# Gates and merge of a hybrid decoder trunk by seven half-size products instead of eight

## The chip, the cores and the metric

The kernel runs on one core of a Trainium2 chip. The metric is the device time of one execution in microseconds, the median of three runs. The core has a matrix engine (PE), a vector engine (DVE), a scalar engine (ACT), a general one (Pool), and a queue engine (SP) that issues the transfers between memory and the on-chip buffers.

## What is computed

Two decoder layers on x of 1024 tokens by 1024 channels, all in float32. Four mixers (stick-breaking attention, S5, retention, RG-LRU) work on slices of one input projection; this change concerns the gates, the merge weights and what surrounds them:

```python
h = _rms_norm(x, pre_g)
proj = jnp.einsum('bsd,dc->bsc', h, w_in)
sb_qkv, ssm_u, ret_qkv, lru_u, gates, merge = jnp.split(proj, SPLITS, axis=-1)
# y_sb, y_ssm, y_ret, y_lru from the first four parts
mix = jnp.stack([y_sb, y_ssm, y_ret, y_lru], axis=2).astype(dtype)
mix = mix * jax.nn.silu(gates.reshape(bsz, s, N_BRANCH, BRANCH_WIDTH))
y = jnp.einsum('bsnw,nwd->bsnd', mix, w_branch)
gate = jax.nn.sigmoid(merge.reshape(bsz, s, N_BRANCH, D_MODEL))
merged = jnp.sum(gate * y, axis=2)
out = jnp.einsum('bsd,de->bse', merged, w_out)
return x + _rms_norm(out, post_g)
```

The gates have 4 x 256 columns and the merge weights 4 x 1024, so together 40 tiles of 128 columns out of 1024 channels.

## The kernel before

The work is cut into four units: two layers times two chunks of 512 tokens. A unit streams 64 weight tiles, called fillers: 16 projections (`i < 16`), then for each of the four mixers a group of ten (two gate tiles, eight merge tiles that carry the branch projection of the same columns), then eight tiles of the output projection. A gate or merge tile is 1024 channels by 128 columns; its product with the normalised chunk is 8 k-slices of 128 channels, and each slice takes three passes, since float32 is made of a high and a low float32r part on both sides: high x high, low x high, high x low (`mm3`). Each pass is one matmul of 128 rows by 512 columns, and a tile fills one PSUM bank with 24 of them (`coltile`, and `filler` for the merge).

Weight tiles come through `load_to` (L178), three tiles ahead, into four raw buffers; `split_to` makes the high part on ACT (L86) and the low part on DVE (L89), three half tiles ahead. Every engine works through its queue in the order in which the program was written: the scheduling is manual, and SP issues all transfers in one queue. Position in a unit is counted in halves of fillers, 128 per unit. The mixers and other side tasks are generators that take their steps at the halves listed in the table `PLAN`:

- `prep` builds the S5 tables of a layer, mostly on Pool (L432, L436). Its longest part doubles the rotation tables `tcos` and `tsin` up to 128 columns, with a scratch buffer. In unit 0 it runs from half 2, in unit 1 for the next layer from half 66.
- `prologue_t` (unit 0) and `prologue` (other units) normalise the next unit's chunk; they square the elements, sum, take 1/sqrt, scale, and split into `hh` and `hl`. In unit 0 this starts at half 96.
- `lru`, `s5`, `ret` and `sba` are the mixers; `post` adds the residual.

General buffers come from a ring of 36 (`genp`, shown as g), accumulators from 3 PSUM banks (pa) and 5 (pb). A buffer's new user waits until the last reader of its old content is done, whichever engine that is on. After the two q tiles of a unit, ACT makes 16 copies from PSUM and 8 more within the buffers, in one piece, ahead of the next weight split in its queue.

## Time and profile before

| | us |
|---|---|
| median of three runs | 1898.11 |
| lowest and highest run | 1894.95, 1898.5 |
| span of the profiled execution | 1895.3 |
| PE busy | 1838.7 (97%) |
| DVE busy | 1180.3 (62%) |
| ACT busy | 903.4 (48%) |
| Pool busy | 252.1 (13%) |
| memory traffic of SP's queue | 192.38 MB, 29.6% of 16 engines |

A busy time counts the recorded length of instructions. Matmuls overlap, so their price is read from the distance of their starts. A time for one engine means little until one knows who waits for it: idle time of an engine that nobody waits for costs nothing.

### The profile page before, as it was taken

Reading aid. Unit: us, or ns where it says so; the run is one execution under the profiler, and the core shown is the slowest. Engines: PE = TensorE matmul, PEld = TensorE weight load, DVE = VectorE, ACT = ScalarE, POOL = GpSimd, SP = SyncE. Lnnn points to the kernel's source line nnn. Section 1 sums busy time; section 2 is a strip of 40 time slices with the busy share of each in tenths; the row PEclk is TensorE's granted clock in tenths of the full one; section 3 lists DMA queues with packets and bytes.
Section 4 is the critical chain, followed back from the end, with each engine's and each line's share of the span. In section 5 each row is a group of like instructions: output and inputs, shape, how many; then the busy total and the mean of one; then the engine's idle time right before and its main releaser. Section 6 shows DMA issues by size and latency. Waiting matters only on the chain.

```text
span 1895.3 us, 24847 instructions
## 1 busy us (share of the span) xinstructions
PE 1838.7 (97%) x9210; PEld 1506.0 (79%) x9210; DVE 1180.3 (62%) x2101; ACT 903.4 (48%) x1733; POOL 252.1 (13%) x579
## 2 busy tenths in 40 slices
PE   8979999999989999979999999999999899999997
PEld 6768888888878878858888788888888788888886
DVE  7667755454669676735547956655537694776454
ACT  5862443344476443524446744344353855344333
POOL 7872000020000002880300000000000000000001
PEclk9989999999999999989999999999999999999999
DMA  5231232324332221314234313232243322212222
GB/s 181 90 104 56 68 117 98 122 93 152 106 117 95 100 72 58 108 47 150 96 127 156 115 69 109 78 137 99 90 136 131 103 98 87 81 68 78 97 98 105
DMA packets 68857, 193.96 MB, mean 102 GB/s; under 512 B 9600, under 2 KB 18176, under 8 KB 68736
## 3 DMA queue, kind: packets, MB, share of 16 engines
q1 hardware_dynamic: 68736, 192.38, 29.6%
q8 instruction: 72, 1.18, 0.2%
q14 instruction: 49, 0.40, 0.1%
HBM read 179.11 MB, written 12.58 MB: 101 GB/s over the span
## 4 chain that ended last, share of the span: by engine, by line
PE 83%; POOL 8%; ACT 4%; DVE 3%; issue 2%; DMA 0%; SPq 0%; DVEq 0%; POOLq 0%; ACTq 0%
PE pa L101 66%; PE pb L101 15%; POOL g L432 4%; ACT g L86 2%; PE pb L1020 2%; POOL psc L436 1%; DVE g L89 1%; POOL tcos L432 1%; POOL tsin L432 1%; POOL g L436 1%; ACT g L83 1%; DVE wl L89 1%; ACT wh L86 0%; DVE g L98 0%; PE pb L253 0%
## 5 line engine op out<-in xcount | busy, mean ns | idle before, releaser
L101 PE MATMUL pa<-hh,wh 128*128 128x512 f32 x1576 | 629.5, 399 | 27.4 <-ACT wh L86 27.4
L101 PE MATMUL pa<-hh,wl 128*128 128x512 f32 x1576 | 617.6, 392 | 8.0 <-DVE wl L89 8.0
L101 PE MATMUL pa<-hl,wh 128*128 128x512 f32 x1576 | 617.5, 392 | 0.0
L89 DVE TENSOR_TENSOR wl<-raw,wh 128x512 fp32r<-128x512 f32 (+1 forms) x512 | 373.8, 768 | 225.7 <-ACT wh L86 225.2
L89 DVE TENSOR_TENSOR g<-g,g 128x512 f32<-128x512 f32 (+7 forms) x432 | 296.0, 685 | 124.5 <-ACT g L86 104.6
L101 PEld LDWEIGHTS pa<-hh,wh 128*128 128x128 f32 x1576 | 298.9, 190 | 90.9 <-ACT wh L86 29.7
L86 ACT ACTIVATE wh<-raw 128x512 fp32r<-128x512 f32 (+1 forms) x512 | 328.2, 685 | 86.6 <-PE pb L101 41.0
L101 PEld LDWEIGHTS pa<-hh,wl 128*128 128x128 f32 x1576 | 298.0, 189 | 74.2 <-DVE wl L89 10.6
L101 PEld LDWEIGHTS pa<-hl,wh 128*128 128x128 f32 x1576 | 298.6, 189 | 58.4 <-DVE hl L89 0.2
L83 ACT ACTIVATE g<-pa 128x512 f32<-128x512 f32 x161 | 96.2, 597 | 501.0 <-PE pa L101 464.6
L89 DVE TENSOR_TENSOR g<-g,pa 128x512 f32<-128x512 f32 x128 | 87.6, 684 | 185.1 <-PE pa L101 165.8
L101 PE MATMUL pa<-g,wh 128*128 128x512 f32 x544 | 169.2, 391 | 3.6 <-DVE g L98 3.4
L86 ACT ACTIVATE g<-pb 128x512 f32<-128x512 f32 (+4 forms) x163 | 72.6, 472 | 145.8 <-PE pb L101 87.8
L906 POOL MEMSET g<- 128x512 f32 x8 | 4.0, 526 | 949.0 <-PE pb L101 947.8
L101 PEld LDWEIGHTS pa<-g,wh 128*128 128x128 f32 x544 | 102.1, 188 | 28.0 <-DVE g L98 5.0
L86 ACT ACTIVATE g<-g 128x512 fp32r<-128x512 f32 (+2 forms) x152 | 79.1, 521 | 61.7 <-DVE g L89 31.8
L86 ACT ACTIVATE g<-pa 64x128 fp32r<-64x128 f32 (+3 forms) x214 | 86.4, 404 | 45.2 <-PE pa L101 42.8
L101 PE MATMUL pa<-g,wl 128*128 128x512 f32 x272 | 106.1, 390 | 0.0
L83 ACT ACTIVATE g<-pb 128x512 f32<-128x512 f32 (+4 forms) x203 | 87.8, 513 | 22.8 <-PE pb L101 20.1
L101 PE MATMUL pa<-wh,g 128*128 128x512 f32 x256 | 79.6, 392 | 0.0
L101 PE MATMUL pb<-wh,g 128*128 128x512 f32 x256 | 79.2, 391 | 0.0
L89 DVE TENSOR_TENSOR g<-pa,g 128x512 f32<-128x512 f32 x51 | 35.7, 703 | 54.6 <-ACT g L83 34.8
(207 smaller groups left out, 2086.4 us busy)
## 6 DMA issues: line engine op xcount, KB each, us to landing
raw<-in_ws_dram SPq DMA_DIRECT2D x128, 640.0 KB, 3.8
raw<-in_ws_dram SPq DMA_DIRECT2D x127, 512.0 KB, 3.6
g<-x SPq DMA_DIRECT2D x32, 256.0 KB, 6.1
g<-in_xt_dram SPq DMA_DIRECT2D x16, 256.0 KB, 6.0
g<-in_x_dram SPq DMA_DIRECT2D x16, 256.0 KB, 3.1
x<-g SPq DMA_DIRECT2D x16, 256.0 KB, 2.1
out_dram<-g SPq DMA_DIRECT2D x16, 256.0 KB, 2.0
g<-in_rot_dram SPq DMA_DIRECT2D x8, 256.0 KB, 4.4
```

What stands on the lines that cost most here:

```text
L83: act.activation(out, in_, func, **kw)
L86: act.activation(out, in_, AF.Copy, **kw)
L89: dve.tensor_tensor(out, a, b, op=op)
L101: pe.matmul(out, lhsT=lhsT, rhs=rhs, start=start, stop=stop)
L432: pool.tensor_tensor(out, a, b, op=op)
L436: pool.tensor_scalar(out, a, s1, None, op0=op0)
L906: pool.memset(t, 0.0)
L1020: pe.transpose(ps[:, q * P:(q + 1) * P], r[:, q * P:(q + 1) * P], ident)
```

## The change

The 40 gate and merge tiles of a layer are taken as 20 pairs, and each pair is computed for both chunks of the layer at once, as a product of two-by-two blocks: two column tiles, two halves of the channels, two chunks of tokens. In place of eight block products there are seven, in the form that uses four sums of weights (s1 to s4) and four sums of tokens (t1 to t4). Each product is 4 k-slices of three passes, 12 matmuls.

- A layer's first unit now runs 12 projections, five `x` stages, four projections, five more `x` stages, twenty `y` stages, and the output projection. `x` makes two products each for two pairs; `y` makes three products for one pair, adds the earlier ones on DVE and does the branch projection. The second unit runs `z` stages (two products each for two pairs), `g` and `m` stages (gating and branch projection) and the output projection. Products and gates that are needed later are written to memory (`late`, `put_late`) and read back (`fetch`).
- `build` makes the sums of tokens on DVE and splits all of them; it follows the normalisation of the second chunk, which thereby moves from half 96 to half 24 in unit 0 (task `tb`). The splits are written to memory and read back (`load_set`).
- `wsums` makes the sums of weights in memory: SP copies a block of weights (1.31 MB) and Pool issues transfers that add another block to it, 32 in all, each behind the landing of the one it depends on.
- The `hp` buffers go; the ring of general buffers has 56, and 8 raw buffers hold tiles of 512 columns, loaded ten ahead. The pass of `mm3` is unchanged.
- Half of the q copies go to DVE, and the eight copies within buffers are put off by one half (`hooks`). The first unit's squares move from Pool to ACT and DVE. The transposed copies of `prologue` are made in pieces of 128 columns. The LRU's low weights are padded to all 128 rows.
- `PLAN` is rewritten for the new positions.

```diff
...
-    hp = ctx.enter_context(tc.tile_pool(name="hp", bufs=1))
-    rawp = ctx.enter_context(tc.tile_pool(name="rawp", bufs=4))
+    rawp = ctx.enter_context(tc.tile_pool(name="rawp", bufs=NRAW))
...
+        if u % 2 == 0:
+            x = [("x", *q) for q in ps]
+            f = p[:12] + x[:XA] + p[12:] + x[XA:] + [("y", q) for q in qs]
+        else:
+            z = [("z", *q) for q in ps]
+            m = [[("m", n, i) for i in range(4)] for n in range(4)]
+            f = p[:12] + z[:ZA] + p[12:] + z[ZA:8] + [("g", 0), z[8]] + m[0][:2] + [z[9], ("g", 1)] + m[0][2:] + m[1][:3]
+            f += [("g", 2), m[1][3]] + m[2][:3] + [("g", 3), m[2][3]] + m[3]
...
+    def ahead(s):
+        load_to(s + NRAW + 2)
+        split_to(s + 3)
...
+            b12, b22 = hc[k], hc[4 + k]
+            t1, t2 = G(), G()
+            tt(t1, b1[k].bitcast(F32), b1[4 + k].bitcast(F32), ALU.add)
+            tt(t1, t1, b12, ALU.subtract)
+            stt(t2, t1, -1.0, b22, ALU.mult, ALU.subtract)
+            yield 0
+            put("t1", t1, True)
...
             if k < 4:
                 sqs.append(G())
-                pool.tensor_tensor(sqs[k], xk[k], xk[k], op=ALU.mult)
-                if k:
-                    pool.tensor_tensor(sqs[0], sqs[0], sqs[k], op=ALU.add)
+                actv(sqs[k], xk[k], AF.Square)
...
+    def prod(ps, s, t, more=False):
+
+        for k in range(4):
+            mm3(ps, s, k * P, P, False, (t[k], t[4 + k]), not more and k == 0, k == 3, more)
...
+    def fetch_y(u, n):
+        drain(("lru", "s5", "ret", "sb")[n])
+        put_late()
+        for j in range(2):
+            S["yf", n, j] = fetch(yd[n][j], u)
...
+            for k in range(3):
+                half(s + k)
+                ps = A()
+                prod(ps, s + k, S[("t2", "t3", "t4")[k]])
+                t = G()
+                tt(t, ps, v, ALU.add)
+                v = t
+                if k < 2:
+                    late.append(((u2d, u3d)[k][j], t))
...
-            for q_, qd, _, _, z in todo:
+            for q_, _, _, _, z in todo:
                 copy(q_, z, scale=0.125)
-                copy(qd, z, scale=0.125)
+            for _, qd, _, _, z in todo:
+                ts(qd, z, 0.125)
...
+        def add(a, b):
+            pool.dma_start(a, b, accum_op=ALU.add, max_dma_last_dim=5120)
+
+        for n in order(2 * l):
+            s1, s2, s3, s4 = (wsum[l][j][n] for j in range(4))
+            sp.dma_start(s3, wq[l, n, 2])
+            sp.dma_start(s2, wq[l, n, 3])
+            yield 0
+            add(s3, wq[l, n, 0])
+            yield 0
+            add(s2, s3)
...
-NGEN = 36
+NRAW = 8
+XA = 5
+ZA = 3
+NGEN = 56
...
```

Three places of the new order matter below. The first is ACT's queue in unit 0, at the tile after the twelfth projection. Before, splits and the rotary copies stood there (wh is a weight's high part, pa a PSUM bank):

```order
L86 ACTIVATE wh_1135<-raw_998 128x512
L86 ACTIVATE wh_1151<-raw_1052 128x512 [waits DMAHW6_49]
L86 ACTIVATE g_1169<-pa_1132 32x512 [waits PE_49]
L86 ACTIVATE g_1169<-pa_1132 32x512 x3
L86 ACTIVATE wh_1181<-raw_1052 128x512
L86 ACTIVATE wh_1197<-raw_1133 128x512 [waits DMAHW1_49,Activation_49]
```

Now the four squares of the second chunk stand there (L83, g_1419 to g_1427), and the first of them waits for Pool, whose doubling used that buffer as scratch:

```order
L86 ACTIVATE g_1408<-pa_1358 128x512 [waits PE_49]
L86 ACTIVATE wh_1412<-raw_1065 128x512 [waits DMAHW3_49,Activation_49]
L83 ACTIVATE g_1419<-g_1378 128x512 [waits DMAHW2_49,Pool_49]
L83 ACTIVATE g_1421<-g_1379 128x512 [waits DMAHW3_49]
L83 ACTIVATE g_1424<-g_1380 128x512 [waits DMAHW4_49]
L83 ACTIVATE g_1427<-g_1381 128x512 [waits DMAHW5_49]
L86 ACTIVATE g_1442<-pa_1359 128x512 [waits PE_49]
```

The copy of pa_1359, which frees that bank for PE, now stands behind the squares.

The second is SP's queue in unit 1, the second half of the groups. Before, it held loads of the next chunk and weight tiles, freed by DVE:

```order
L229 DMA g_7835<-x_113 128x512 [waits DMAHW3_49]
L229 DMA g_7836<-x_113 128x512 [waits DMAHW4_49]
L264 DMA g_7820<-in_preg_dram 128x512 [waits DMAHW5_49,PE_49]
L264 DMA g_7821<-in_preg_dram 128x512 [waits DMAHW6_49,PE_49]
L178 DMA raw_7858<-in_ws_dram 128x1280 [waits DMAHW7_49,DVE_49]
L178 DMA raw_7914<-in_ws_dram 128x1280 [waits DMAHW0_49,DVE_49]
```

Now it holds spilled products (u, ge, go), mixer results (y) and small weight tiles; g_8668 takes the scratch of the next layer's doubling:

```order
L1211 DMA g_8662<-ge_212 128x512 [waits DMAHW5_49,DMAHW3_49]
L1211 DMA g_8664<-go_232 128x512 [waits DMAHW4_49,PE_49]
L363 DMA y_0_251<-g_8625 128x512 [waits DVE_49]
L363 DMA y_1_252<-g_8626 128x512 [waits DMAHW6_49,Activation_49]
L1211 DMA g_8668<-y_0_249 128x512 [waits DMAHW7_49,Pool_49]
L1211 DMA g_8670<-y_1_250 128x512 [waits DMAHW0_49]
L217 DMA raw_8674<-in_wb_dram 128x512 [waits DMAHW1_49]
L1211 DMA g_8686<-u_8_175 128x512 [waits DMAHW2_49]
L1211 DMA g_8688<-u_9_176 128x512 [waits DMAHW3_49,PE_49]
L217 DMA raw_8705<-in_wb_dram 128x512 [waits DMAHW4_49,DVE_49]
```

The wait for Pool stands ahead of the loads of u_8, u_9 and of all weight tiles that follow.

The third is Pool's queue in unit 0, after the doubling, in the steps that make the chunk inputs' tables. Before:

```order
L432 TENSOR_TENSOR g_1386<-g_446,g_272 128x8x16
L432 TENSOR_TENSOR g_640<-g_640,g_272 128x128 [waits Pool_49]
L432 TENSOR_TENSOR g_1386<-g_1386,g_640 128x8x16 [waits Pool_49]
L432 TENSOR_TENSOR g_1387<-g_640,g_272 128x8x16 [waits DMAHW6_49]
L432 TENSOR_TENSOR g_640<-g_446,g_272 128x128 [waits Pool_49]
L432 TENSOR_TENSOR g_1387<-g_1387,g_640 128x8x16 [waits Pool_49]
L432 TENSOR_TENSOR g_1386<-g_446,g_272 128x8x16
L432 TENSOR_TENSOR g_640<-g_640,g_272 128x128 [waits Pool_49]
```

Now two transfers that add in memory stand among these steps, the second behind the landing of the first; these rows are the end of that stretch:

```order
L503 TENSOR_TENSOR g_1960<-g_672,g_479 128x8x16
L503 TENSOR_TENSOR g_865<-g_865,g_479 128x128 [waits Pool_49]
L503 TENSOR_TENSOR g_1960<-g_1960,g_865 128x8x16 [waits Pool_49]
L503 TENSOR_TENSOR g_1961<-g_865,g_479 128x8x16
L503 TENSOR_TENSOR g_865<-g_672,g_479 128x128 [waits Pool_49]
L503 TENSOR_TENSOR g_1961<-g_1961,g_865 128x8x16 [waits Pool_49]
L1610 DMA ws_1_0_119<-ws_2_0_123 256x1280 [waits DMASW0_49]
L503 TENSOR_TENSOR g_1960<-g_672,g_479 128x8x16
L503 TENSOR_TENSOR g_865<-g_865,g_479 128x128 [waits Pool_49]
L503 TENSOR_TENSOR g_1960<-g_1960,g_865 128x8x16 [waits Pool_49]
```

The steps below the transfer, and those of ACT and DVE that read their results, stand behind that landing.

## Rows read from the trace of the kernel before

**Rows 1.** The page: span, and busy time of each engine.

```profile
span 1895.3 us, 24847 instructions
...
PE 1838.7 (97%) x9210; PEld 1506.0 (79%) x9210; DVE 1180.3 (62%) x2101; ACT 903.4 (48%) x1733; POOL 252.1 (13%) x579
```

**Rows 2.** Timeline of PE at 500 us: start, us, engine, line, operation.

```profile
499.67 0.39 PE L101 MATMUL pa<-hh,wl 128*128 128x512 f32 x1
499.90 0.39 PE L101 MATMUL pa<-hh,wh 128*128 128x512 f32 x1
500.13 0.39 PE L101 MATMUL pa<-hl,wh 128*128 128x512 f32 x1
```

**Rows 3.** Chain of waits, one piece at 892 us: start, us, what.

```profile
892.48 27.22 PE pa L101 x120
```

**Rows 4.** Waits of PE, whole span: us in total, times, longest.

```profile
PE pa L101 <- ACT wh L86: 27.4, 5, 13.4
```

**Rows 5.** The page, costliest groups: one of three passes; count, busy us, mean ns.

```profile
L101 PE MATMUL pa<-hh,wh 128*128 128x512 f32 x1576 | 629.5, 399 | 27.4 <-ACT wh L86 27.4
```

**Rows 6.** Timeline of PE after its longest stops; idle time and releaser in brackets.

```profile
95.02 0.50 PE L101 MATMUL pa<-hh,wh 128*128 128x512 f32 x1 [2.30 <-ACT wh L86]
...
119.12 0.79 PE L101 MATMUL pa<-hh,wl 128*128 128x512 f32 x1 [7.82 <-DVE wl L89]
...
568.92 0.80 PE L101 MATMUL pa<-hh,wh 128*128 128x512 f32 x1 [5.14 <-ACT wh L86]
...
848.38 0.80 PE L101 MATMUL pa<-hh,wh 128*128 128x512 f32 x1 [13.41 <-ACT wh L86]
```

**Rows 7.** Timelines of ACT, Pool and DVE around the S5 tables of both layers.

```profile
95.52 2.40 ACT L86 ACTIVATE g<-pa 32x512 f32<-32x512 f32 x4
...
115.11 1.26 POOL L432 TENSOR_TENSOR tsin<-tsin,g 128x512 f32<-128x512 f32 x1
...
116.41 0.69 DVE L89 TENSOR_TENSOR g<-pa,g 128x512 f32<-128x512 f32 x1 [14.70 <-POOL tsin L432]
...
118.39 1.28 DVE L89 TENSOR_TENSOR wl<-raw,wh 128x512 fp32r<-128x512 f32 x2
...
846.62 1.08 ACT L86 ACTIVATE g<-pb 128x512 f32<-128x512 f32 x2 [23.47 <-POOL tsin L432]
```

**Rows 8.** Stretches: us, busy us of each engine (instructions), PEclk, DMA share, GB/s.

```profile
20.00:118.00 98.00, 86.86 (x382) 68.19 (x380) 60.52 (x120) 71.05 (x149) 85.72 (x235) 0.98 0.24 83
758.30:847.90 89.60, 76.67 (x406) 62.78 (x405) 45.54 (x68) 33.68 (x62) 79.22 (x206) 0.95 0.21 74
10.00:15.00 5.00, 2.03 (x9) 1.37 (x9) 5.00 (x4) 4.42 (x8) 4.84 (x4) 1.00 1.05 397
10.00:20.00 10.00, 6.97 (x29) 5.16 (x29) 10.00 (x10) 8.61 (x15) 9.84 (x8) 1.00 0.96 361
```

**Rows 9.** Rows by shape of DVE and ACT: count, busy us, mean ns.

```profile
L89 DVE TENSOR_TENSOR wl<-raw,wh 128x512 fp32r<-128x512 f32 x256 | 171.4, 700 | 113.0 <-ACT wh L86 112.5
L89 DVE TENSOR_TENSOR g<-g,g 128x512 f32<-128x512 f32 x232 | 166.5, 718 | 14.7 <-ACT g L83 7.2
L89 DVE TENSOR_TENSOR g<-g,pa 128x512 f32<-128x512 f32 x128 | 87.6, 684 | 185.1 <-PE pa L101 165.8 <-ACT g L83 18.5 <-PE pb L1020 0.7
...
L1058 DVE TENSOR_TENSOR_SCAN g<-g,ec,ones 128x511 f32<-128x511 f32 x32 | 41.1, 1283 | 0.0
...
L98 DVE SCALAR_TENSOR_TENSOR g<-g,ss,g 128x512 f32<-128x512 f32 x26 | 19.3, 745 | 0.0
L98 DVE SCALAR_TENSOR_TENSOR g<-pa,g 64x128 fp32r<-64x128 f32 x64 | 18.5, 289 | 25.6 <-ACT g L86 23.8
...
L83 ACT ACTIVATE g<-g 128x512 f32<-128x512 f32 x44 | 25.8, 625 | 22.8 <-DVE g L89 18.0 <-POOL g L432 4.6
```

**Rows 10.** Page: SP queue (packets, MB, share); a weight load (us to landing).

```profile
q1 hardware_dynamic: 68736, 192.38, 29.6%
...
raw<-in_ws_dram SPq DMA_DIRECT2D x127, 512.0 KB, 3.6
```

## What I expect of the change

> **What bounds the kernel now.** I read the page first, then the waits of PE, the timeline of PE, the rows by shape, and last the waits and rows of the other engines at the places that the change touches. The page shows one engine nearly full: PE is busy for 97% of the span [rows 1]. A busy share says little about matmuls that overlap, so the reader should look at their starts: 512-column matmuls start every 0.226 to 0.23 us (499.67, 499.90, 500.13), though each is shown as 0.39 long [rows 2]. The pitch is their price; over a run of 120 that follow each other in the chain of waits it is 27.22 / 120 = 0.2268 us [rows 3]. PE waits for others for some 45 us in all, of which 27.4 us for ACT's splits, in five waits [rows 4]. DVE is busy for 62% [rows 1]. So PE work that goes is time that goes, unless something now hidden comes out.
>
> **The matmuls that go.** Two 128-column tiles of gate or merge weights over two chunks of tokens cost 2 x 2 x 24 matmuls (8 k-slices, three passes). The seven products cost 7 x 12 (4 k-slices, three passes). That is 96 against 84 for each of 20 pairs in two layers, so 480 matmuls fewer: 480 x 0.2268 = **-108.9 us**, all of it from the group in [rows 5] and the two like it for the other passes. The row padding of the LRU's weights and the wider mask matmul differ by a few us of either sign; I take +2. PE: **-107**.
>
> **Waits that go.** In unit 1, 13.41 us of PE's idle time end with ACT [rows 6], and ACT had waited 23.47 us for Pool's tsin [rows 7]. The part of the S5 tables that caused it is now given other places: -13. After the q tiles of each second chunk PE stands for 5.14 us, at 568.92 [rows 6] and again at 1503.78, while ACT makes sixteen copies and more; half of them are moved to DVE and the rest are put behind the next weight split: 2 x 5.1 = -10. Together **-23**.
>
> **New wait in unit 0.** The normalisation of the second chunk (prologue_t) starts at half 24, where it stood at half 96. Its first square on ACT takes over the scratch buffer of Pool's table doubling, so ACT's queue stands until the doubling is done. In the trace Pool works on these tables almost without a gap, 85.7 of 98 us [rows 8], and its last tsin ends at 115.1 + 1.3 = 116.4 us [rows 7]. The tile of halves 24 and 25 had its first copies on ACT at 95.52 [rows 7]; less its 24 matmuls and the wait of 2.30 us at 95.02 [rows 6], half 24 began at about 87 us. Three products of 12 matmuls bring PE to about 95, where it needs a bank that ACT has not read; ACT's queue opens at 116.4 and takes four squares of 0.63 us before that read [rows 9], so PE goes on at about 119: a stall of 24 us. The kernel before lost 7.8 us there, seen at 119.12 [rows 6]. The seven squares and adds that `first` takes from Pool may bring Pool's end forward by up to 7 us; Pool's seven sums of squares then delay the statistics that PE reads by a few us. Bounds +8 and +20; I take **+13**.
>
> **New wait in unit 1.** SP's queue now holds a load of the S5 result whose buffer is the same scratch, in the middle of the merge stage: SP cannot issue it before the doubling is over, and behind it stand the loads of two spilled products and all weight tiles. Pool needs from 758.3 to 847.9 us, 89.6 us, after the exponent's tail [rows 8]; that tail stands at half 59 now, and PE runs out of loaded operands at about half 73, 14 halves later. By the counts of the part on DVE below, 24 halves of this stage take 80 us on PE and 101 on DVE, so 14 take 47 to 59 us, and the stall is 31 to 43 us. Pool's stretch has 79.2 us of work in it; if its waits go, the lower end is 20. I take **+28**, bounds 20 and 43.
>
> **Pool's queue.** The weight sums are DMAs that add in memory, issued by Pool and each waiting for a landing. Two of them stand among the table steps of unit 0, and ACT and DVE wait for steps behind them at halves 45 and 46. Nothing of the kind is in the trace. The nearest row from below is a 512 KB load that lands in 3.6 us [rows 10]; the sums are 1.31 MB, 2.5 times as much, so 9 us for each if nothing overlaps. Bounds 0 and 18; I take **+7**.
>
> **DVE.** Counted from the new instruction order by the durations of [rows 9], DVE gets about 176 more additions that read PSUM (0.684 us), 35 of SBUF tiles (0.718), 40 scaled ones (0.745) and 96 copies of 64 or 128 columns (0.289): 120 + 25 + 30 + 28 = some 200 us on 1180. That is under 1840 in total, so by the mean it is hidden. By stages it is not: in halves 64 to 87 of units 1 and 3 there are 40 PSUM additions, 36 SBUF ones, 35 splits and the scans, 27 + 26 + 25 + 23 = 101 us, against 300 matmuls and 89 small ones, 80 us. Two splits of 0.70 take 1.28 together [rows 7], 0.91 of their sum, so 101 is some 93. In the q tiles' stage it is 33 against 24. So DVE exceeds PE by 13 + 9 = 22 us in each of two units, 44 in all. In unit 1 the 13 lie under SP's stall, and three halves that are split ahead, some 9 us, are used up first in each unit: 44 - 13 - 18 = 13. Bounds 0 and 44; I take **+15**.
>
> **DMA.** The products, the sums of tokens and the sums of weights are put into memory and read back. Payload grows from 192 MB [rows 10] to some 440 MB. At most the queue moved 397 GB/s over 5 us and 361 over 10 us [rows 8]. In unit 0, halves 40 to 71 hold 127 transfers of 0.262 MB, 4 copies and 4 sums of 1.31 MB: 43.8 MB, or 49 if a sum counts twice. That is 110 to 136 us, against 384 matmuls and 140 small ones, some 103 us. By the same count the last 32 halves of the y stage need 93 to 131 us against 88, unit 2's halves 40 to 71 need 104 to 126 against 99, and its y end 86 to 117 against 88; other stages fit. The sum of what does not fit is 17 to 130 us. Two of four sums are not read before the next unit, and weights are loaded ten tiles ahead; a stall elsewhere also gives the queue time. Bounds 0 and 130; I take **+25**, close to the lower end, because the rate at which a sum reads its target appears in no row.
>
> On this the Trainium skill speaks against the change. "DMA: Bandwidth & Descriptors", section Issuing engines are not separate DMA queues, says that transfers from SP and Pool run on the same 16 engines and interleave; here all but a sliver of packets came from one queue, so no run shows it. "Collectives: The Full Stack", section The bandwidth ceiling: the fold count and why AG ≠ RS ≠ AR, says that a reduction is slow because an addition needs two source reads; by that rule the upper ends above would apply, and the time would be the second rival's. No run here shows it.
>
> **The sum.** 1895.3 - 107 - 23 + 13 + 28 + 7 + 15 + 25 = 1853. The median lies 2.8 us above the profiled span, so **1856 us**.
>
> **Rivals.** (1) *The stalls are hidden and the whole saving comes through.* Pool ends its tables earlier than before (it has lost the squares), SP's blocked load finds operands already loaded, and the memory traffic fits: 1895.3 - 107 - 23 + 8 + 20 + 0 + 0 + 0 = 1793, with the median's 2.8 us 1796; with up to 30 us of the other terms left, 1796 to 1826. For it speaks that PE waited only 45 us in all before and that most buffers are more numerous (56 for 36, 8 raw for 4). Against it speaks Pool's continuous stretch [rows 8]. (2) *The DMA engines become the bound.* If a sum occupies the engines twice and copies from memory to memory run no faster than 361 GB/s, the stages above wait 130 us instead of 25: 1856 + 105 = 1961. It makes the kernel slower as soon as the stages wait more than 25 + (1902 - 1856) = 71 us. For it speaks that the queue's demand exceeds the best rate seen in four stages; against it, that PE's longest waits in the trace end with ACT and DVE, not with a transfer [rows 6]. (3) *The saved matmuls do not shorten PE's time*, because the seven products run in half-length groups of 12 with a new bank each: against it, the 120 matmuls of [rows 3] run over several banks at the same pitch. I give it little; 0.2 us lost at each of 280 products would be 56 us, 1912.
>
> **How the numbers follow.** Forecast (1826 to 1886) 0.47; rival 1 0.24; rival 2 0.18; rival 3 and other mixtures above 1886 0.11, of which 0.03 are still faster, 0.05 within 0.2% and 0.03 slower. Of the time outside the range, about 0.05 lies below and 0.13 above, which gives 1795 to 1945. About 0.2% of the time, 4 us, is what a measurement can tell from no change. Faster: 0.24 + 0.47 + 0.03 = 0.74; same 0.05; slower 0.21.
>
> **What would show it.** Right: PE's 512-column matmuls are 480 fewer at an unchanged pitch; a PE gap of 15 to 25 us around 95 to 120 us that ends with ACT, whose wait names Pool; an SP wait for Pool of some tens of us in unit 1's merge stage, with PE idle behind it; DVE over 90% busy in that stage. Wrong: the pitch rises; PE's waits end with DMAs in units 0 and 2, or ACT's splits wait for raw tiles there (rival 2); no gap over 10 us (rival 1).

## The result, and the profile after

The changed kernel takes 2160.78 us in the median of four runs (2154.18 to 2166.76) against 1897.23 us in four runs of the kernel before (1894.95 to 1898.5): 1.139 times as long, 95% interval 1.1362 to 1.1419. The forecast was 1856 us (1826 to 1886), and the time lies above the range and on the other side of the time before.

First the page of the changed kernel: span, busy times, the two DMA queues (packets, MB, share of 16 engines; q1 is SP's, q0 is Pool's), and of its issues those of the weight sums (count, KB each, us to landing).

```profile
span 2156.5 us, 27173 instructions
...
PE 1828.5 (85%) x8730; PEld 1480.7 (69%) x8730; DVE 1361.6 (63%) x2496; ACT 924.7 (43%) x1825; POOL 275.2 (13%) x605
...
q1 hardware_dynamic: 216432, 416.84, 56.3%
q0 software_dynamic: 8704, 41.95, 9.9%
...
ws<-in_wq_dram POOLq DMA_DIRECT2D x16, 1280.0 KB, 13.4
ws<-ws POOLq DMA_DIRECT2D x16, 1280.0 KB, 12.6
```

The matmuls are 480 fewer than in [rows 1], 8730 for 9210, as the arithmetic says; PE is busy for 85% where it was for 97%. So the matmuls are saved, and PE stands still for much more than they took. Who it waits for, over the whole span (us in total, times, longest):

```profile
PE pb L1091 <- DVE g L89: 105.8, 28, 12.2
PE pa L1189 <- DVE g L89: 101.1, 37, 11.3
PE pa L1189 <- ACT g L86: 42.3, 8, 14.2
PE pa L1189 <- DMA g<-xs_t: 25.0, 9, 5.8
```

Before, the one large row was 27.4 us [rows 4]. The matmuls of L1189 are the seven products and all other passes of `mm3`, those of L1091 the small ones of the attention. The first two rows name DVE, which is busy for only 63%; the reader should not stop at them but ask what DVE had waited for. Part of the answer is a transfer (waits of DVE):

```profile
DVE g L89 <- DMA g<-ge: 56.0, 13, 10.4
DVE g L89 <- DMA g<-y: 32.1, 7, 12.4
DVE g L89 <- DMA g<-u: 16.3, 2, 14.0
```

ge, y and u are values that are read back from memory. Nearly all of the waits for ge and y fall in units 0 and 2, whose `y` stages fetch them; u is fetched by the `z` stages, and 14.0 of its 16.3 us are one wait in unit 1 (see the scratch buffer below). Stretches of 50 us in the `y` stages of units 0 and 2 show what holds them up (columns as in [rows 8]: us, busy us of PE, PEld, DVE, ACT, Pool, clock, DMA share, GB/s; the share adds up the times of packets, so it can pass 1):

```profile
450.00:500.00 50.00, 39.01 (x175) 31.17 (x173) 26.64 (x42) 10.72 (x19) 2.14 (x3) 0.90 1.05 317
...
1500.00:1550.00 50.00, 34.89 (x158) 27.70 (x156) 20.54 (x33) 10.62 (x19) 2.68 (x3) 0.89 1.04 315
1550.00:1600.00 50.00, 41.65 (x164) 33.76 (x165) 26.49 (x42) 8.81 (x15) 2.68 (x3) 0.87 1.04 291
```

The DMA engines are full (1.04 and 1.05), at 291 to 317 GB/s where 361 to 397 were seen before [rows 8]; PE is busy for 35 to 42 of 50 us. That is the second rival's picture. It is not the whole of it: in units 1 and 3 no weight sums are made, yet more than half of the lost time lies there.

To place the loss I laid the starts of PE's instructions against the program's order and took, for every eight halves, the time beyond pitch times count. The kernel before has some 56 us of such time in all. After:

| unit | 0 | 1 | 2 | 3 | sum |
|---|---|---|---|---|---|
| us beyond PE's pitch | 129 | 124 | 60 | 107 | 420 |

420 - 56 = 364 more lost time, less 107 for the matmuls: 257 of the 261 us by which the span is longer. The pitch of the small matmuls is uncertain: other choices of it move both sums by some tens of us, single units by up to 20, and the difference by under 10. In the new order units 0 and 2 have 164 halves (the `y` stages are 72 to 147), units 1 and 3 have 104 (`z` stages from 24, the output projection from 88).

### The profile page after: what moved, and what is told of

Read it like the earlier page. It is cut to its first block, busy times and chain, and to the rows that moved or that the text cites. A ratio compares the mean times of both kernels' runs of the same rounds, so it can differ in the third digit from the quotient of the medians.

```text
span 2156.5 us, 27173 instructions
## 1 busy us (share of the span) xinstructions
PE 1828.5 (85%) x8730; PEld 1480.7 (69%) x8730; DVE 1361.6 (63%) x2496; ACT 924.7 (43%) x1825; POOL 275.2 (13%) x605
## 3 DMA queue, kind: packets, MB, share of 16 engines
q0 software_dynamic: 8704, 41.95, 9.9%
## 5 line engine op out<-in xcount | busy, mean ns | idle before, releaser
L1189 PE MATMUL pa<-g,wh 128*128 128x512 f32 x3376 | 1107.5, 410 | 171.0 <-DVE g L89 95.6
L1189 PEld LDWEIGHTS pa<-g,wh 128*128 128x128 f32 x3376 | 655.2, 198 | 331.2 <-issue 90.1
L1189 PE MATMUL pa<-g,wl 128*128 128x512 f32 x1688 | 681.7, 404 | 10.8 <-DVE wl L89 10.8
L89 DVE TENSOR_TENSOR wl<-raw,wh 128x512 fp32r<-128x512 f32 x536 | 369.1, 695 | 348.3 <-ACT wh L86 342.2
L1189 PEld LDWEIGHTS pa<-g,wl 128*128 128x128 f32 x1688 | 332.2, 197 | 87.1 <-DVE wl L89 14.2
L86 ACT ACTIVATE wh<-raw 128x512 fp32r<-128x512 f32 x536 | 324.6, 623 | 156.6 <-PE pa L1189 53.9
L83 ACT ACTIVATE g<-g 128x512 f32<-128x512 f32 (+2 forms) x218 | 133.0, 618 | 592.7 <-DVE g L89 530.4
L89 DVE TENSOR_TENSOR g<-pa,g 128x512 f32<-128x512 f32 x227 | 156.5, 690 | 212.3 <-PE pa L1189 135.7
L1189 PE MATMUL pa<-wh,g 128*128 128x512 f32 x448 | 141.6, 398 | 6.3 <-DVE g L89 5.5
L1091 PE MATMUL pb<-cons,g 128*128 128x128 f32 x288 | 51.6, 315 | 106.1 <-DVE g L89 105.8
L86 ACT ACTIVATE g<-pa 32x512 f32<-32x512 f32 (+3 forms) x190 | 92.6, 487 | 91.1 <-PE pa L1189 62.7
L1091 PEld LDWEIGHTS pb<-cons,g 128*128 128x128 f32 x288 | 37.3, 159 | 118.5 <-issue 112.5
L1189 PE MATMUL pb<-wh,g 128*128 128x512 f32 x320 | 100.3, 395 | 5.2 <-ACT g L86 5.2
L1189 PEld LDWEIGHTS pa<-wh,g 128*128 128x128 f32 x448 | 84.3, 191 | 27.1 <-DVE g L89 8.7
L83 ACT ACTIVATE g<-pb 128x512 f32<-128x512 f32 (+4 forms) x203 | 87.5, 510 | 13.6 <-PE pb L1189 7.5
L1189 PE MATMUL pa<-wl,g 128*128 128x512 f32 x224 | 88.4, 395 | 0.1
## 6 DMA issues: line engine op xcount, KB each, us to landing
ws<-in_wq_dram POOLq DMA_DIRECT2D x16, 1280.0 KB, 13.4
ws<-ws POOLq DMA_DIRECT2D x16, 1280.0 KB, 12.6
```

The source lines that it names most:

```text
L83: act.activation(out, in_, func, **kw)
L86: act.activation(out, in_, AF.Copy, **kw)
L89: dve.tensor_tensor(out, a, b, op=op)
L1091: pe.transpose(ps[:, q * P:(q + 1) * P], r[:, q * P:(q + 1) * P], ident)
L1189: pe.matmul(ps, lhsT=a, rhs=b, start=start and i == 0, stop=stop and i == 2, skip_group_check=more)
```

## Experiments

Each kernel differs from the changed one, or from another experiment where that is said, by the edit shown, cut to its main lines. Times are medians of two runs (four for the three that were run last on the changed kernel, ten for the last of all), beside a kernel before of 1896 to 1897 us. "Loses" means time beyond PE's pitch, as in the table.

**The scratch buffer.** The doubling gets a buffer of its own (the start-up matmuls' operand lends its room), so neither ACT in unit 0 nor SP in unit 1 waits for it.

```diff
-        tmp = G()
+        tmp = ptmp
```

> The scratch of the table doubling gets a buffer of its own, so that no other tile takes it over. Theory (scratch shared): the 21 us for which PE stood in unit 0 behind ACT, and the 26 us for which SP stood in unit 1 behind Pool, go, with the low clock behind them: 2110 to 2125 us. Rival (the ring hands on another buffer that Pool holds as long): within 10 us of the changed kernel's 2160.

Measured: 2152.7 us, the rival's result; its two runs, 2159.2 and 2146.3, lie further apart than the 8 us gained. In the changed kernel the wait was where the prediction put it; timelines of PE, of ACT and of Pool in unit 0 (idle time before, and its releaser, in brackets):

```profile
100.80 1.22 PE L1189 MATMUL pa<-g,wh 128*128 128x512 f32 x2 [6.93 <-ACT g L86]
...
120.34 1.22 PE L1189 MATMUL pa<-g,wh 128*128 128x512 f32 x2 [14.19 <-ACT g L86]
```

```profile
97.49 2.63 ACT L86 ACTIVATE g<-g 64x128 fp32r<-64x128 f32 x8 [4.26 <-DVE g L98]
100.15 0.60 ACT L86 ACTIVATE g<-pa 128x512 f32<-128x512 f32 x1
...
117.61 2.19 ACT L83 ACTIVATE g<-g 128x512 f32<-128x512 f32 x4 [16.21 <-POOL tsin L503]
```

```profile
116.32 1.26 POOL L503 TENSOR_TENSOR tsin<-tsin,g 128x512 f32<-128x512 f32 x1
...
118.85 4.32 POOL L402 TENSOR_TENSOR g<-g,g 128x512 f32<-128x512 f32 x3
123.89 5.70 POOL L402 TENSOR_TENSOR g<-g,g 128x512 f32<-128x512 f32 x4 [0.72 <-ACT g L83]
```

Only the second of PE's stops, 14.19 us, is a wait for the scratch: the squares (117.61) wait for tsin, and the read of PE's bank stands behind them. The first, 6.93 us, has another cause, and the 21 us of the theory had counted it in: ahead of that bank's read (100.15) ACT makes the eight put-off q copies (97.49), which had waited for the q pieces that DVE makes (L98). With the scratch apart this stop stays, at 6.92 us, and so it does in the next experiment, at 6.93.

The last two rows of Pool explain the rest of the miss: Pool also forms the seven sums of squares (L402), behind the doubling in its queue. With the scratch apart, PE waits 17.1 us for these instead (first row: waits of PE in this experiment). In unit 1 SP's wait (second row, of the changed kernel) goes, with it DVE's waits for u, and halves 72 to 79 lose 8.0 instead of 20.3 us.

```profile
PE pb L101 <- POOL g L403: 17.1, 1, 17.1
```

```profile
SPq L1211 <- POOL psc L507: 25.9, 1, 25.9
```

**Both of Pool's parts.** The scratch apart, and the sums of squares on DVE:

```diff
-            pool.tensor_tensor(acc, acc, sq, op=ALU.add)
+            tt(acc, acc, sq, ALU.add)
```

> The changed kernel with the doubling's scratch in a buffer of its own (2152.7 us by itself) and, added to it, the seven sums of squares of the second chunk's normalisation on DVE instead of Pool. With the scratch alone PE's wait moved from ACT's squares to the matmul that needs Pool's sums, 17.1 us. Theory: with both, nothing of the normalisation waits for Pool's tables, so the wait of about 24 us that the prediction placed in unit 0 is gone: 2120 to 2135, and the excess of unit 0's halves 24 to 31 falls by over 15 us. Rival: the wait moves a third time, to the sums of tokens, the attention and the products behind them, as it did when the whole task was put later: within 10 us of 2153.

Measured: 2132.0 us, 28.8 below the changed kernel: unit 0 loses 16 us less, all of it in halves 24 to 31 (15.4 for 31.4), unit 1 loses 11 less. That is the theory's result. The wait was real; in unit 0 it took two edits to remove, because two things stood behind Pool.

**The attention's steps spaced out.** `PLAN` gives the attention's forty steps in units 1 and 3 two halves in three from half 25, where they had stood two, three and four in a row from 31:

```diff
-        "sb": (31, 32, 34, 35, 36, 37, 39, 40, 41, 43, 44, 45, 46, 48, ...),
+        "sb": (24,) + tuple(25 + 3 * i + j for i in range(19) for j in range(2)),
```

> In units 1 and 3 the attention's steps stand at halves 25 + 3i (matmuls) and 26 + 3i (DVE), so DVE has two halves before PE asks for its product; in the changed kernel it mostly has one. Nothing else moves. Theory (products asked for too soon): most of the 98 us in which PE waited for DVE at the transposes of these two units go, and the low clock after each: 2030 to 2090 us. Rival (DVE has too much to do in these stages): the work is the same and starts seven halves earlier, under 25 us gained.

Measured: 2127.0 us, 34 gained, the low edge missed by half. Waits of PE in this run:

```profile
PE pa L1189 <- DVE g L89: 108.9, 38, 13.1
PE pb L1091 <- DVE g L89: 50.5, 21, 8.6
...
PE pb L101 <- DVE g L89: 20.8, 8, 4.2
```

The attention's own row halves (105.8 to 50.5), but 15 us come back at its other matmuls (6.2 to 20.8 at L101) and 8 at the products (101.1 to 108.9). Of the 55 us that position takes from this wait, 23 only move.

**No weight sums.** No copies and no adding transfers; plain blocks are loaded in the sums' places, so those products have other values:

```diff
-            sp.dma_start(s3, wq[l, n, 2])
-            sp.dma_start(s2, wq[l, n, 3])
-            add(s3, wq[l, n, 0])
-            add(s2, s3)
...
```

> Leaves out the sums of weights: no copies and no adding transfers, and the y and z stages load plain blocks in place of the sums (so 126 MB of the DMA engines' payload go, the loads stay). Theory (transfers bound the ends of the y stages): the 48 us in which PE waited for DVE, and DVE for loads of spilled products, at the ends of the two y stages go, with the low clock: 2070 to 2110 us. Rival (those loads are late because of their place in SP's queue): under 25 us gained.

Measured: 2037.7 us, 123 gained, more than theory allowed. Units 0 and 2 fall from 129 and 60 us of lost time to 52 and 12, and PE's waits for xs_t vanish. A stretch of this run in the `y` stages of unit 0:

```profile
430.00:480.00 50.00, 50.00 (x222) 41.44 (x221) 33.43 (x53) 14.89 (x26) 0.00 (x0) 1.00 0.68 221
```

PE is full, with the DMA engines at 0.68.

**Copies kept, additions left out.** SP still copies 32 blocks, Pool adds nothing to them:

```diff
-            add(s3, wq[l, n, 0])
-            add(s2, s3)
...
-            add(s1, wq[l, n, 3])
-            add(s4, s2)
```

> The changed kernel with the copies of weight blocks kept and the 32 adding transfers left out (so the sums are wrong). Leaving out both gained 123 us. Theory (an adding transfer holds the engines about twice as long as a copy of the same size: 9.9% of the engines' time for 42 MB, where 42 MB of the other queue take 5.7%): two thirds of the gain, 2070 to 2090 us. Rival (the copies from memory to memory cost as much as the adding ones): half of it, 2095 to 2105 us. Second rival (what hurts is that Pool's queue stands for the landings): the whole gain, near 2040.

Measured: 2047.4 us. That misses the theory and is the second rival's figure: the 32 adding transfers make 113 of the 123 us, and the copies, of the same size each, some 10 once the others are gone. Whether the cost is Pool's standing queue or the transfers themselves, the next run was made to tell.

**Plain transfers in the place of the additions.**

```diff
-            pool.dma_start(a, b, accum_op=ALU.add, max_dma_last_dim=5120)
+            pool.dma_start(a, b, max_dma_last_dim=5120)
```

> The changed kernel with Pool's 32 adding transfers issued as plain copies of the same blocks at the same places behind the same waits (so the weight sums are not formed and the products that read them have other values). Leaving these 32 out gained 113 us. Theory: what costs is the addition in memory, whose read of the target and slow packets hold the 16 engines 1.75 times as long per byte (42 MB at 196 GB/s against 343 in SP's queue); as plain copies they take about 57% of the engine time and the y stages regain most of their loads' rate: 2050 to 2100. Rival: what costs is that Pool's queue stands behind each landing, or the mere bytes of 32 more transfers; both stay, so 2130 to 2160.

Measured: 2104.2 us (ratio to before 1.1104, 1.1071 to 1.1137), between the theory and the rival: 57 of the 113 us go with the addition, 57 stay with the transfers. The page's row of Pool's queue, and two issue rows:

```profile
q0 software_dynamic: 8704, 41.95, 5.1%
...
ws<-in_wq_dram POOLq DMA_DIRECT2D x16, 1280.0 KB, 10.1
ws<-ws POOLq DMA_DIRECT2D x16, 1280.0 KB, 10.5
```

5.1% of 2105 us is 107 us of all 16 engines, for 41.95 MB; with the addition it was 9.9% of 2156.5 = 213 us, twice as much for the same bytes. From 213 to 107 us of that occupancy brought 57 us, from 107 to none another 57. The second rival of the run before falls: Pool's queue stands ahead of these transfers for 771 us in the changed kernel, and for 710 here, but hardly anyone waits for it. In units 0 and 2 of the changed kernel, where the transfers are issued, SP never waits for Pool, and PE, ACT and DVE wait for it for some 26 us in all, in the first 300 us of unit 0, at the tables and the sums of squares. That the engines' occupancy is the cost is what these numbers leave, not a separate proof; in the second 57 us occupancy and bytes cannot be told apart.

**Three together.** Scratch, spacing and no weight sums:

> The three edits of the other runs together (the sums of weights are left out here too). If the three causes are independent, the gains add up: 1890 to 2005 us. If they hide one another, the time is below the sum of the three gains by more than 30 us; if one takes the place of another, above it.

Measured: 1988.0 us, 173 gained where the three gave 8 + 34 + 123 = 165 singly. They add up. The next four, and the two with work left out further below, start from this kernel.

**Work taken off DVE.** Every second low part of the weights and the merge's additions go to Pool in units 1 and 3:

```diff
+            if cur[0] % 2 and k % 2:
+                copy(his[k], r)
+                pool.tensor_tensor(los[k], r, his[k].bitcast(F32), op=ALU.subtract)
```

> Built on the three edits together (1988 us; sums of weights left out). In units 1 and 3 every other low part of the weights and the additions of the merge go from DVE to Pool, some 60 instructions of 0.7 us in each unit. Theory (in these units DVE has as much to do as PE, 301 us against 295 in halves 8 to 87, and PE waits for its turn): the 185 us that these units take above the pitch of their matmuls fall by 50 to 110, 1880 to 1940 us. Rival (the chain of matmul, ACT, DVE, matmul is too long for the short stages, however busy DVE is): under 25 us gained.

Measured: 1989.6 us, no gain. The two units did not stay as they were, though: unit 3 loses 11 us less, and unit 1, where Pool also has the next layer's tables to make, 13 us more. There PE waits for low parts that Pool makes late (waits of PE):

```profile
PE pa L1195 <- POOL wl L231: 12.2, 2, 10.2
```

So DVE's load costs something, but 11 us in the unit where Pool has time is far from the 25 to 55 per unit that the theory asked for. It falls, as far as Pool is a fair place for the work: the 151 instructions that left DVE are some 106 us at 0.70, but its busy time fell only from 1360.2 to 1328.9, because those that stayed became longer (last section).

**The second chunk later.** Unit 0's task `tb` from half 34 instead of 24:

```diff
-        "tb": (24, 25, 27, 28, 29, 31, ...),
+        "tb": tuple(range(34, 66)),
```

> Built on the three edits together (1988 us; sums of weights left out). In unit 0 the normalisation of the second chunk and the sums of tokens start at half 34 in place of 24, behind the table doubling. Theory (in unit 0 PE waits for Pool's sums of squares, which stand behind the doubling in Pool's queue): the 31 us above the pitch at halves 24 to 31 go, 1955 to 1970 us. Rival (what is moved delays the stage where it lands as much): 1980 or more.

Measured: 1987.1 us, no gain, the rival's result: halves 24 to 31 lose about 12 us instead of 31, and halves 32 to 79 lose some 20 more than before.

**A bank read late.** In `x` and `z` two products share a bank: the first is read out, and the second is accumulated on top. Here the first read moves behind the second product, which gives other values but keeps every instruction:

```diff
-                if k < 2:
+                if k >= 2:
                     v = G()
-                    copy(v, ps[k])
+                    copy(v, ps[k - 2])
```

> Built on the three edits together (1988 us; sums of weights left out). In the x and z stages a pair's second product is added to the first in the same PSUM bank, after ACT or DVE has read the first; one other product lies between. Here the first read is made after the second product, so PE waits for no read within a stage, and all instructions stay (the values read are then wrong). Theory (PE waits for that read, since ACT's and DVE's queues are more than one product late): PE's 50 us of waits for DVE and 21 us for ACT at products fall by two thirds, with the low clock 1915 to 1945 us. Rival (PE is late for DVE in any case and waits at the next bank): under 15 us gained.

Measured: 1955.3 us, 33 gained; theory asked for 43 or more. Waits of PE in this run; in the three-together run the first row was 10.5 us, the second 50.0 and the last 21.0:

```profile
PE pa L1190 <- DVE wl L89: 26.6, 9, 5.4
PE pa L1190 <- DVE g L89: 23.7, 22, 5.0
...
PE pa L1190 <- ACT g L86: 5.6, 4, 1.7
```

The waits for readers fall by 42 us, and 16 of them turn up as waits for the low parts of weights. What such a wait looks like stands in the changed kernel after the q tiles of unit 3, DVE's queue and then PE's:

```profile
1776.36 2.40 DVE L93 TENSOR_SCALAR g<-pa 64x128 fp32r<-64x128 f32 x8
1778.78 2.53 DVE L98 SCALAR_TENSOR_TENSOR g<-pa,g 64x128 fp32r<-64x128 f32 x8
...
1783.98 0.69 DVE L89 TENSOR_TENSOR g<-pa,g 128x512 f32<-128x512 f32 x1
```

```profile
1784.82 1.19 PE L1189 MATMUL pa<-g,wh 128*128 128x512 f32 x2 [9.78 <-DVE g L89]
1785.81 0.63 PE L1189 MATMUL pa<-g,wl 128*128 128x512 f32 x1
1786.24 1.05 PE L1189 MATMUL pa<-g,wh 128*128 128x512 f32 x2
...
1788.19 0.40 PE L1189 MATMUL pa<-g,wl 128*128 128x512 f32 x1
1788.43 0.62 PE L1189 MATMUL pa<-g,wh 128*128 128x512 f32 x2
1788.89 0.40 PE L1189 MATMUL pa<-g,wl 128*128 128x512 f32 x1
```

DVE works without a gap; the read of the bank (1783.98) stands behind the q pieces, a split and the S5's products, and PE waits 9.78 us for it. With the late read this stop is gone (it was 10.10 us in the three-together run), but PE then stops twice a little later:

```profile
1610.04 0.79 PE L1190 MATMUL pa<-g,wl 128*128 128x512 f32 x1 [3.85 <-DVE wl L89]
...
1621.93 1.30 PE L1092 MATMUL pb<-cons,g 128*128 128x128 f32 x5 [7.26 <-DVE g L89]
```

So at this place, behind a queue of DVE that is long whoever waits for it, only 2 us are won. Most of the 33 us come from halves 32 to 39 and 48 to 55 of units 1 and 3, 5 to 6 us each, less 3 to 5 that halves 40 to 47 lose more, and 6 us from unit 2. The Trainium skill ("Perfetto Trace Analysis", section Matmuls) says that independent groups should rotate through different banks so that the reading of one overlaps the next group's matmuls. The two products that share a bank here have a read between them, and this run puts 33 us on that.

**Pairs in threes.** Three pairs in three banks instead of two in two, so that a bank has two products' time to be read; the order of products, loads and spills changes with it:

```diff
-        ps = [(qs[2 * i], qs[2 * i + 1]) for i in range(NQ // 2)]
+        ps = [tuple(qs[i:i + 3]) for i in range(0, NQ, 3)]
...
-            ps = [A(), A()]
+            ps = [A() for _ in range(e)]
```

> Built on the three edits together (1988 us; sums of weights left out). The x and z stages take three tile pairs at a time in place of two, in three banks, so two products lie between a bank's first product and its second, and nothing else changes. Theory (PE waits for the read between the two): most of what the run with the late read gains, 1920 to 1955 us. Rival (with all three banks in use the next stage waits for its first bank instead): under 15 us gained.

Measured: 1987.0 us, no gain: the row on DVE falls from 50.0 to 29.2 us, the one on ACT rises from 21.0 to 34.3, which fits three banks that are all taken when the next user asks for one, the rival.

**The attention's products left out,** on top of the late bank read: DVE's scans and products of the attention in units 1 and 3 are not done.

```diff
-            if i < n:
+            if i < n and c:
+                J[i]["f"] = None
+            elif i < n:
```

> The run with the late read, and in units 1 and 3 the attention's scans and products on DVE are left out too (its matmuls, sigmoids and transposes stay). Theory (the transposes wait for DVE's chain): the 37 us of waits at transposes and the 21 us at logits go, 50 to 80 us below the run with the late read. Rival (these waits come from the logits' banks and from ACT): under 25 us below it.

Measured: 1913.5 us, 42 gained where the theory asked for 50 to 80; units 1 and 3 lose 53 and 48 us instead of 82 and 77. This takes away work and not only a wait, so it is a bound: no placement of the attention can still give more than some 42 us.

**All causes out.** The last kernel, with the sums of squares on DVE too:

> The run with scratch, spacing, weight sums, early bank read and attention products mended or left out (1913.5 us) and, added to it, the seven sums of squares on DVE. Left out of the computation: the weight sums, the scans and products of the attention in units 1 and 3; the banks are read after the second product. Theory: the causes are independent and the ledger closes, so the 20.7 us that the squares gave by themselves come here too: 1890 to 1900, no faster than the kernel before although 480 matmuls (107 us) are gone; what is left are the many stops of a few us of the new stages. Rival: unit 0's wait of 31 us after the q tiles moves to the next work, as it did when the whole task was put later, since PE is here the bound everywhere else: 1908 to 1916.

Measured: 1896.2 us, ratio to before 1.0002 (0.9992 to 1.0012): 17 gained, and with all this mended or left out the kernel is as fast as the one before. Its page:

```profile
span 1896.3 us, 26892 instructions
...
PE 1790.5 (94%) x8730; PEld 1440.8 (76%) x8730; DVE 1262.5 (67%) x2311; ACT 918.8 (48%) x1821; POOL 234.9 (12%) x566
```

**The q copies as before,** on the changed kernel:

```diff
-            for _, qd, _, _, z in todo:
-                ts(qd, z, 0.125)
+                copy(qd, z, scale=0.125)
...
```

> The changed kernel (2160.8 us) with the q tiles' copies as before: all sixteen from PSUM on ACT, and the eight copies within buffers in the same piece instead of half a tile later. The prediction took 10 us of gain from moving them. Theory: that gain did not come, because in units 1 and 3 the q tiles' stage now has its waits on DVE (about 20 us each above PE's pitch in halves 24 to 31, also where everything else is mended), and DVE's scaled copies are part of that; with ACT doing them again the time falls to 2135 to 2155, and the excess of those halves goes below 14 us each. Rival: the move did gain what the prediction said, so undoing it costs: 2165 to 2180, with waits for ACT after the q tiles in all four units.

Measured: 2155.7 us (ratio 1.1373, 1.1356 to 1.139; the changed kernel's interval overlaps it). Neither theory nor rival: the move gained nothing that shows, and the halves behind the q tiles still lose 17 us in units 1 and 3 (20 with the move). Waits for ACT's wh, 11.0 us, come back for those that go. The stop that was 9.78 us in unit 3 is as long as before:

```profile
1778.48 1.19 PE L1189 MATMUL pa<-g,wh 128*128 128x512 f32 x2 [10.02 <-DVE g L89]
```

**Sums by Pool, on chip.** Two versions replace the adding transfers by additions on Pool. The first adds all four sums in the loaded tiles, with doubled loads for `z`, and has the scratch, the spacing and the later second chunk too:

```diff
+            if len(ts_) > 1:
+                ptt(ts_[0], ts_[0], ts_[1], ALU.add)
...
+                ptt(raws[k - 1], raws[k - 1], raws[k - 2], ALU.add)
+                ptt(raws[k - 2], raws[k], raws[k - 1], ALU.add)
```

> Nothing is left out. The sums of weights are made by Pool in the buffers, from plain blocks: a y stage loads blocks 0, 2 and 3 and makes both of its sums from them, a z stage loads twice as many tiles as before; no sum goes through memory. With the scratch of its own, the spaced attention and the second chunk at half 34. Theory (the traffic of the sums was the cost, not the sums): as the run with the second chunk later, 1955 to 1995 us. Rival (Pool's additions come too late, or slow DVE): 2010 or more.

Measured: 2061.6 us, the rival's result. Against the run with the later second chunk most of the loss is in units 1 and 3, whose `z` stages now load twice as many tiles: 29 and 24 us. The second adds in the `y` stages only, stores two sums once for the next unit, and takes the threes and the other repairs with it:

```diff
+                ptt(s1, b, c, ALU.add)
+                ptt(b, b, a, ALU.add)
+                ptt(a, c, b, ALU.add)
+                ptt(d, d, a, ALU.add)
+                pend.extend(((k, wss(l, 0, q), s1), (k, wss(l, 3, q), d)))
```

> Nothing is left out. Scratch of its own, spaced attention, groups of three, and the sums of weights by Pool in the y stages from the blocks that are loaded there; the two sums that the next unit needs are stored once, without copies or adding transfers. Theory (the traffic of adding transfers, the attention's spacing and the read between the products are the main costs): 1935 to 1985 us, still above the kernel before. Rival (Pool's additions slow DVE or come late): 2010 or more.

Measured: 2055.2 us, again the rival's; the `y` stages lose 39 us in unit 0 and 24 in unit 2 again. With the same scratch and spacing the adding transfers would give some 2119 by the single gains (2160.8 - 8 - 34), so adding on Pool is better; but both are far from the 1988 us without sums. No version that does all the work comes near the kernel before.

## Why the prediction was wrong, point by point

**PE's work: right.** 480 matmuls fewer; 512-column matmuls still start every 0.23 us (1788.19, 1788.43, 1788.89 for one, two and one in the timeline above: 0.70 us for three), so rival 3 is out: no product of 12 loses pitch by itself.

**Unit 0's wait for Pool: right in mechanism, too high.** ACT's queue opened at 117.6 us, forecast 116.4; PE went on at 120.3, forecast 119. But PE stood there for 14.2 us and not for 24, since it came to that bank at 106 and not at 95: the stop of 6.93 us before it, which the q copies make, was in no term. Taking both of Pool's causes away gave 16 us in those halves, some 8 net of the old stall of 7.8, where +13 was taken: the lower bound. The step put the sums of squares in Pool's queue at a few us, and by themselves they hold PE for 17.1.

**Unit 1's wait for Pool: right in place, too high.** SP waited 25.9 us, where the stall was put at 28; but only 11 to 12 us of it reached PE.

**Pool's queue: not shown apart.** +7 was taken. ACT waits once, 5.1 us, for these table steps; halves 40 to 47 of unit 0 lose some 5 us, almost nothing without weight sums, but some 8 with only the additions left out. No run ties this to the landings.

**The q copies: wrong.** The 10 us did not come. In units 1 and 3 the wait changed its name, from ACT's split to DVE's read of a bank. The eight copies that DVE now makes ahead of that read are not what makes it long: with all of them on ACT the stop is 10.02 us instead of 9.78. In unit 0 the put-off copies make a stop of 6.93 us, 5.2 with the copies as before. The wait of 13 us in unit 1 that ended with ACT is gone, as forecast.

**DVE: the count was right, the conclusion not.** Halves 64 to 87 of unit 3 and of unit 1:

```profile
1983.90:2098.80 114.90, 89.31 (x436) 69.64 (x435) 88.53 (x150) 38.98 (x73) 0.00 (x0) 0.90 0.58 197
936.80:1067.40 130.60, 94.42 (x452) 73.96 (x451) 92.44 (x150) 48.48 (x98) 63.97 (x160) 0.86 0.55 188
```

DVE's work there is 88.5 and 92.4 us, forecast 93. But the stage takes 115 to 131 us, so DVE is busy for 71 to 77%, not over 90%, and PE for 72 to 78%. Neither engine is full: they wait for each other in turn. A sum of busy times by stage cannot show that; the order of the queues does. Two such chains were never priced, because the prediction looked at each engine's load and at new waits for Pool only: the attention's steps in units 1 and 3 (34 us by position, at most some 42 more) and the second product in a bank that has still to be read (33 us). Together they are as large as the miss of the DMA term.

**DMA: of the terms with a price, the one that failed most.** +25 was taken between 0 and 130; the weight sums alone cost 123 (additions 113, copies 10), near the upper end. The arithmetic of the stages was right: the `y` ends of units 0 and 2 were named, and they are where the loss is. The choice was wrong: the value was put near the lower end "because the rate at which a sum reads its target appears in no row", which is a reason for the middle or for a wider range, not for an end. The Trainium skill's rule that was set against the change fits. "Collectives: The Full Stack", section The bandwidth ceiling: the fold count and why AG ≠ RS ≠ AR, has an addition cost two source reads, there for collectives in a ring; the trace agrees in size, 213 us of the engines against 107, though no view shows the second read itself. "DMA: Bandwidth & Descriptors", section Issuing engines are not separate DMA queues, has transfers of Pool and SP interleave on the same engines. The trace agrees: without Pool's additions DVE's waits for ge, which SP loads, fall from 56.0 to 7.4 us.

**The second rival was right in mechanism and near in price:** it put the stages' wait at 130 us, and 123 went with the weight sums. Its 1961 us was too low because of the waits above that neither it nor the forecast had. It had the sign that the prediction named, PE's waits ending with DMAs in units 0 and 2, though most of them pass through DVE first.

**The clock was in no term.** Mean granted clock of before and of after:

```profile
core 0: 1895.3 us, clock 0.987
```

```profile
core 0: 2156.5 us, clock 0.924
```

After the 9.78 us stop above, PE's matmuls start 0.43 us apart (1785.81 to 1786.24), then 0.23 again from 1788.19. The granted clock is 0.51 from 1785 to 1788, the level of 1.2 GHz, and 1.00, that of 2.4, in the next 3 us. Eight matmuls took 3.37 us (1784.82 to 1788.19) where 1.8 would do, so the stop cost some 1.6 us more than its 9.78. Of all 512-column matmuls, some 510 start 0.3 to 0.52 us before the next one, the distance seen at the low clock, where some 300 did before; beyond 0.228 each they take some 82 us, 33 before. These 49 us are contained in the 364 and in the parts above.

**What stays open.** From 2160.8 to 1896.2 the ledger is: three together 173, the late bank read 33, the attention's products 42, the squares 17. Three of these leave work out or change values, so they show what the waits cost and not what a repair would give. The last kernel still loses some 160 us beyond PE's pitch, 104 more than the kernel before, which is all that the matmuls had saved. It lies in many stops of 1 to 9 us: about 20 us in halves 24 to 31 of units 1 and 3 each, 8 to 9 in halves 80 to 87, some 17 in the output projection of unit 1, 41 in unit 0. Their causes were not told apart one by one. So of the 305 us between forecast and result the runs trace some 265. The last 40 stay open, and with them the 65 that the forecast had granted, net, to waits of its own: the 104.

## What to carry to other kernels

On a kernel whose main engine is 97% busy, fewer instructions on that engine are worth their price only if each stage's other resources still fit; here 107 us of matmuls were exchanged for 266 MB more memory traffic, 395 more DVE instructions and a shared accumulator, and even with every named cause out, and work left out with some of them, the exchange came to nothing. Price an unseen operation by the bound that its mechanism gives, not by the lack of a row, and ask of each accumulator how many instructions stand in the reader's queue between the last matmul and the read. A busy share of 63% does not mean that an engine answers at once.

## What the runs showed of the hardware

- A transfer that adds in memory held the DMA engines twice as long as the same transfer without the addition: 213 us against 107 for 41.95 MB, that is 196 against 391 GB/s. One of 1.31 MB landed 12.6 to 13.4 us after its issue, a plain one in its place 10.1 to 10.5. The bytes on the page are equal in both kernels, so only the share shows the difference.
- Additions on Pool lengthened DVE's instructions with two operands in SBUF and not those that read PSUM. In the three-together run and then in the run with all sums on Pool (count, busy us, mean ns):

```profile
L89 DVE TENSOR_TENSOR g<-g,g 128x512 f32<-128x512 f32 x267 | 189.8, 715 | 15.9 <-ACT g L83 7.1 <-DMA g<-y 2.0
L89 DVE TENSOR_TENSOR g<-pa,g 128x512 f32<-128x512 f32 x227 | 156.5, 690 | 160.5 <-PE pa L1190 126.9 <-ACT g L86 29.2 <-ACT g L83 4.1
```

```profile
L89 DVE TENSOR_TENSOR g<-g,g 128x512 f32<-128x512 f32 x267 | 214.0, 806 | 16.3 <-ACT g L83 6.9 <-DMA g<-y 2.5
L89 DVE TENSOR_TENSOR g<-pa,g 128x512 f32<-128x512 f32 x227 | 156.2, 689 | 128.4 <-PE pa L1203 96.8 <-ACT g L86 23.0 <-ACT g L83 7.9
```

  715 became 806 ns, 690 stayed 689. "SBUF — State Buffer" in the Trainium skill, section Who interferes with whom, says that instructions of DVE with two SBUF inputs contend with Pool's that read SBUF; the trace agrees. It is part of why work moved to Pool gained little: in the run that took 106 us of work off DVE, its busy time fell by 31.
- A wait that was given another place in the program came back in full (1987.1 for 1988.0 us with the second chunk later, 1987.0 with pairs in threes), while three causes that were taken out added up almost exactly (165 us singly, 173 together).
